# Attention values as two float16 parts with a power-of-two scale per feature, in place of three bfloat16 parts: eight products a head in place of twelve

## The chip, the cores and the metric

The kernel runs on one core of one Trainium2 chip, in one launch. The metric is the device time in microseconds (us) of one execution. Engines are named as in the profile: PE is TensorE (its weight loads are shown apart, as PEld), DVE is VectorE, ACT is ScalarE, POOL is GpSimd and SP is SyncE, which issues most of the DMAs. Each engine works through its own list of instructions in order.

## The reference, cut to what matters

Two layers work on 256 tokens of width 2048 beside 256 context tokens. Layer 0 is a Fourier mixer, layer 1 is attention with 64 query heads over 8 key/value heads of 64 features. The change touches the values of layer 1 alone.

```python
def _attend_with_sink(q, k, v, sink, mask=None):
    s = jnp.einsum('bqhgd,bkhd->bhgqk', q, k).astype(jnp.float32) * (ATTN_HEAD_DIM ** -0.5)
    if mask is not None:
        s = jnp.where(mask, s, NEG_INF)
    sk = jnp.broadcast_to(sink.astype(jnp.float32)[None, :, :, None, None], s.shape[:-1] + (1,))
    p = jax.nn.softmax(jnp.concatenate([s, sk], axis=-1), axis=-1)[..., :-1]
    return jnp.einsum('bhgqk,bkhd->bqhgd', p.astype(v.dtype), v)
...
    y = jnp.moveaxis(o, 0, 1).reshape(b, n, D_BRANCH) * jax.nn.silu(z)
```

All is float32. After attention comes `x + gate * (y @ w_out[1])` and a last norm.

## The kernel before

**Split products.** A float32 product is made of reduced parts. `mm3` (L77 to L80) forms one product of two matrices, each held as a high and a low part (`h`, `l`, or `wh`, `wl`), with three matmuls into one accumulator. The high part is a cast on ACT (L65), the low part a subtraction on DVE (L66). Weights come in 1 MB pieces into `raw` (three buffers) and are split half by half into the pool `ws` (six buffers, so three pairs `wh`, `wl`).

**Keys and values.** With the normed inputs `hx1` (tokens) and `hc1` (context), 32 rounds of products give, for each of four blocks of 128 tokens (`tb` 0 and 1 are tokens, 2 and 3 context), a tile of keys and one of values in PSUM; this takes all eight PSUM buffers. Then the keys of the tokens are rotated (`roped`, L879 to L885, on DVE), those of the context are copied (L941, ACT), and each values tile is split into three bfloat16 parts: a cast on ACT (L930), the rest on DVE (L931), a cast of the rest (L932), a second rest on POOL (L934). The tile `va` (list `v01`) holds parts one and two side by side for each of the eight key/value heads, 64 + 64 columns; `vb` (list `vlo`) holds the third part beside 64 zero columns (L933). At last PE turns the keys (L946, 16 transposes of 128x128) into `kT`.

**The heads.** A loop of 66 turns runs over the 64 query heads. Head i, in `stage_s`, makes its scores with four matmuls of 128x512 (L1134, L1135), takes a masked row maximum on DVE (L1136), the exponential on ACT (L1139), and the scaled probabilities as two float16 parts side by side in `f` (L1146 on ACT, L1147 on DVE). Two DMA transposes (L1148, issued on SP) put `f` into `ft` (three buffers). `stage_o`, two turns later, multiplies `ft` with the values: for each of four key blocks there are three matmuls of 128x256 (L1156: parts one and two times the high probabilities; L1157: the same times the low ones; L1158: part three times the high ones). Rows 0 to 63 and 64 to 127 of the result are added (L1163, L1164), and `emit_y` (L1119) scales by 0.5/PS and gates it.

**What fills PE meanwhile.** Each turn has two slots (`filler`), which take the next unit of a list: the query projections (`q`, 8 units a key/value head), the gate projections (`z`, two units a block) and, once these are used up, 12 units of the output projection (`o`). Ten units run before the first head. A q or z unit is 12 or 16 matmuls; an o unit is half as long. So the last six heads have about half of the filling work of the others.

**What sets the order.** The program is written in this order, but a scheduler with a cost model of its own rearranges it at build time and fixes the order of each engine. A few places are pinned by `issue_after`. The tile pools set when a buffer can be written again.

Of the kernel before, what the change touches and what calls it, by code (L numbers as in the profile page):

```python
# [10 lines left out]
F32 = mybir.dt.float32  # L11
F32R = mybir.dt.float32r
F16 = mybir.dt.float16
BF16 = mybir.dt.bfloat16
AF = mybir.ActivationFunctionType
ALU = mybir.AluOpType
AX = mybir.AxisListType

P = 128
# [4 lines left out]
N = 256  # L24
G = 16
GD = 256
EPS = 1e-6
PS = 32768.0


@with_exitstack
def tile_dit(ctx: ExitStack, tc: tile.TileContext, a: dict, out: bass.AP):
    nc = tc.nc
    V, S, PE, GP = nc.vector, nc.scalar, nc.tensor, nc.gpsimd
# [3 lines left out]
    wsp = ctx.enter_context(tc.tile_pool(name="ws", bufs=6))  # L38
    actp = ctx.enter_context(tc.tile_pool(name="act", bufs=33))
# [3 lines left out]
    def psum():  # L43
        return pp.tile([P, 512], F32, tag="ps", name="ps")
# [9 lines left out]
    def act(dt=F32):  # L54
        return actp.tile([P, 512], dt, tag="act", name="act")
# [44 lines left out]
    ident = const.tile([P, P], F32, name="ident")  # L100
# [452 lines left out]
    for g in range(G):  # L553
# [9 lines left out]
        elif g == 4:  # L563
            w = []
            for kh in range(2):
                with tc.issue_after((mix0, mix1)[kh]):
                    v, m = fold_uh(load_uh(g, kh), g, kh)
# [3 lines left out]
        elif g > 4:  # L571
# [3 lines left out]
            v = f3[1][0]  # L575
# [123 lines left out]
    with tc.tile_pool(name="yp", reuse_waits="tile", bufs=32) as ypool:  # L699
# [20 lines left out]
        with tc.tile_pool(name="zp", reuse_waits="tile", bufs=2) as zp:  # L720
# [30 lines left out]
            for b in range(4, NB):  # L751
# [3 lines left out]
                o = psum()  # L755
# [41 lines left out]
        for i in range(32):  # L797
            sw, kg = i // 16, i % 16
            if kg == 0:
                o = [psum() for _ in range(8)]  # L800
# [6 lines left out]
            if kg >= 12:  # L807
                for k in range(sw * 8 + (kg - 12) * 2, sw * 8 + (kg - 12) * 2 + 2):
                    t = act()
# [41 lines left out]
    with tc.issue_after(st_end[0]):  # L851
        o = psum()
# [33 lines left out]

    with tc.tile_pool(name="h1", reuse_waits="tile", bufs=16) as h1p:
        hx1 = []
        v01, vlo = [], []
        kT = []  # L890
        with tc.tile_pool(name="kvp", reuse_waits="tile", bufs=2) as kvp:
            hc1 = []
            for k in range(KT):
                hx = h1p.tile([P, 512], F32R, tag="h1", name="h1")
                hc = kvp.tile([P, 512], F32R, tag="h1c", name="h1c", bufs=16)
                t = kvp.tile([P, 512], F32, tag="ht", name="ht")
                for s, h in ((0, hx), (1, hc)):
                    q = slice(s * N, (s + 1) * N)
                    V.scalar_tensor_tensor(t[:, q], x1[k][:, q], gs1[:, k, s : s + 1], r_bc1[:, q] if k else r_ps[s], op0=ALU.mult, op1=ALU.mult)
                    a_ = S.activation(h[:, 0:N], t[:, q], AF.Identity, bias=sh1[:, k, s : s + 1]).ins  # L900
                    if s == 0:
                        a_end = a_
                    e = V.scalar_tensor_tensor(h[:, N : 2 * N], t[:, q], sh1[:, k, s : s + 1], h[:, 0:N].bitcast(F32), op0=ALU.add, op1=ALU.subtract).ins
                if k == 0:
                    h_end = [e] + [S.copy(r_bc1[:, i * N : (i + 1) * N], r_ps[i]) for i in range(2)]
                    with tc.issue_after(bc_end), tc.issue_after(a_end):
                        x1_turn(0, 3)
                        x1_turn(1, 3)
                hx1.append(hx)
                hc1.append(hc)  # L910
            o = [[psum() for _ in range(2)] for _ in range(4)]
            for kg in range(8):
                with tc.issue_after(h_end[0]), tc.issue_after(sq_end[0]):
                    w = ws_split(raw(a["wkv"][kg])) if kg else [w0, half_split(wr, 1)]
                for j in range(2):
                    k = kg * 2 + j
                    wh, wl = w[j]
                    for tb in range(4):
                        h = (hx1, hc1)[tb // 2][k]
                        c = (tb % 2) * P  # L920
                        for kv in range(2):
                            q = slice(kv * 512, (kv + 1) * 512)
                            mm3(o[tb][kv], h[:, c : c + P], h[:, N + c : N + c + P], wh[:, q], wl[:, q], k == 0, k == KT - 1)
            kr = []
            for tb in range(4):
                src = o[tb][1].rearrange("p (h d) -> p h d", d=64)
                va, vb = (actp.tile([P, 8, P], BF16, tag="act", name="v") for _ in range(2))
                rest = act()
                rv = rest.rearrange("p (h d) -> p h d", d=64)
                S.copy(va[:, :, 0:64], src)  # L930
                V.tensor_tensor(rv, src, va[:, :, 0:64], op=ALU.subtract)  # L931
                S.copy(va[:, :, 64:128], rv)  # L932
                GP.memset(vb[:, :, 64:128], 0.0)  # L933
                GP.tensor_tensor(vb[:, :, 0:64], rv, va[:, :, 64:128], op=ALU.subtract)  # L934
                v01.append(va)
                vlo.append(vb)
                t = kvp.tile([P, 512], F32, tag="kr", name="kr", bufs=4)
                if tb < 2:
                    roped(t, o[tb][0], tb, kvp)
                else:  # L940
                    S.copy(t, o[tb][0])  # L941
                kr.append(t)
            for hp in range(4):
                o = psum()
                for tb in range(4):
                    PE.transpose(o[:, tb * P : (tb + 1) * P], kr[tb][:, hp * P : (hp + 1) * P], ident)  # L946
                t = act()
                S.copy(t, o)
                kT.append(t)


        y1 = []
        raw1, fin = [None], []
        oA, curw, kg1, yh = [], [None], [0], []
        with tc.tile_pool(name="at", reuse_waits="tile", bufs=2) as at:

            kk, qq, obs, szs = {}, {}, {}, {}
# [155 lines left out]
            def emit_y(blk):  # L1113
                if blk not in szs or (blk, 1) not in obs or blk in ydone:
                    return
                ydone.add(blk)
                if blk % 2 == 0:
                    y1.append(act())
                V.scalar_tensor_tensor(y1[blk // 2][:, (blk % 2) * N : (blk % 2 + 1) * N], obs[blk, 1], 0.5 / PS, szs.pop(blk), op0=ALU.mult, op1=ALU.mult)  # L1119

            def stage_s(i):
                hk, blk, hh = i // 8, i // 2, i % 2
# [28 lines left out]
            def stage_o(i, ft):  # L1151
                hk, blk, hh = i // 8, i // 2, i % 2
                oo = psum()
                for kb in range(4):
                    fh, fl = (ft[:, j, :, :].rearrange("p t q -> p (t q)") for j in (kb, 4 + kb))
                    PE.matmul(oo[:, 0:N], v01[kb][:, hk, :], fh, start=kb == 0, stop=False)  # L1156
                    PE.matmul(oo[:, 0:N], v01[kb][:, hk, :], fl, start=False, stop=False)  # L1157
                    PE.matmul(oo[:, 0:N], vlo[kb][:, hk, :], fh, start=False, stop=kb == 3)  # L1158
                if hh == 0:
                    obs[blk, 0] = at.tile([P, N], F32, tag="ob", name="ob", bufs=4)  # L1160
                ob = obs[blk, 0]
                t = at.tile([64, N], F32, tag="ot", name="ot", bufs=1)
                S.copy(t, oo[64:128, 0:N])  # L1163
                V.tensor_tensor(ob[hh * 64 : hh * 64 + 64, :], oo[0:64, 0:N], t, op=ALU.add)  # L1164
                if hh == 1:
                    obs[blk, 1] = ob
                    emit_y(blk)
# [27 lines left out]
        with tc.tile_pool(name="fin", reuse_waits="tile", bufs=1) as fp:  # L1195
# [31 lines left out]
            o = [[psum() for _ in range(2)] for _ in range(2)]  # L1227
# [182 lines left out]
```

## Time and profile before

| | |
|---|---|
| median of 3 runs | 1826.32 us (1824.57 to 1828.72) |
| the profiled execution | 1825.82 us, its span 1823.8 us |
| PE busy | 1783.1 us (98%) |
| DVE busy | 1407.4 us (77%) |
| ACT busy | 900.6 us (49%) |
| key and value products end | about 1115 us |
| first head's scores, last head's values product | 1156 us, 1665 us |

Times in the trace count from the start of the span. A row of a timeline gives the start and the duration in us, the engine, the line and what is written from what; a bracket gives the idle time of the engine before it and who ended it. A PE row's duration includes its pipeline, so what a matmul costs in a dense stretch is the distance from one start to the next. In a table of groups, "x256 | 71.3, 279 | 12.0" is 256 instructions, 71.3 us busy, 279 ns each, and 12.0 us of idle time just before them. A table by windows gives for each stretch the busy time of each engine, the granted clock of PE, and the busy share of the DMA engines.

### The profile page before, as it was taken

What the parts mean: (1) busy time and instruction counts of PE and PEld (TensorE: products, weight loads), DVE (VectorE), ACT (ScalarE), POOL (GpSimd) and SP (SyncE); (2) the same over time, 40 slices, a digit from 0 to 9 for tenths busy, and PEclk for the clock granted to TensorE, in tenths of its full rate; (3) what the DMA queues carried; (4) which work ended last, traced back from release to release, by engine and by line L of the source; (5) the groups of instructions that cost most, each with busy time, mean ns of one, the idle gap of its engine ahead of it and who ended that gap; (6) DMA issues with size and microseconds to landing.
All of it is one profiled execution on the core that took longest, in us unless ns stands there. A gap on an engine that the chain in (4) does not pass through costs nothing. (4 is left out here: it accounts for less than half of the span.)

```text
span 1823.8 us, 26431 instructions
## 1 busy us (share of the span) xinstructions
PE 1783.1 (98%) x9661; PEld 1501.0 (82%) x9661; DVE 1407.4 (77%) x2774; ACT 900.6 (49%) x1535; POOL 187.0 (10%) x193
## 2 busy tenths in 40 slices
PE   6999999999999999999999999999999999997997
PEld 4679999888888888888888888788888888886886
DVE  5779888887879887767874745889889988995455
ACT  5545444522222243324322534788778877875343
POOL 0001112000000000000000002203221220300001
PEclk9999999999999999999999999999999999998999
DMA  9988889665766647653566333687888798986553
GB/s 395 417 326 236 232 242 254 220 223 225 259 237 242 241 170 294 245 208 118 193 255 257 117 113 117 185 205 191 200 203 203 200 207 193 247 199 194 187 183 138
DMA packets 209473, 399.93 MB, mean 219 GB/s; under 512 B 156288, under 2 KB 156688, under 8 KB 174272
## 3 DMA queue, kind: packets, MB, share of 16 engines
q1 hardware_dynamic: 185280, 360.24, 61.7%
q0 software_dynamic: 19920, 31.06, 6.8%
q10 hardware_dynamic: 4144, 6.95, 1.1%
q8 instruction: 76, 1.25, 0.3%
q14 instruction: 53, 0.43, 0.1%
HBM read 352.06 MB, written 12.59 MB: 200 GB/s over the span
## 5 line engine op out<-in xcount | busy, mean ns | idle before, releaser
L65 ACT CAST wh<-raw 128x1024 fp32r<-128x1024 f32 x333 | 348.9, 1049 | 565.1 <-PE ps L79 447.6
L66 DVE TENSOR_TENSOR wl<-raw,wh 128x1024 fp32r<-128x1024 f32 x333 | 422.6, 1271 | 240.5 <-ACT wh L65 237.1
L79 PE MATMUL ps<-act,wh 128*128 128x512 f32 x1024 | 398.2, 389 | 0.0
L78 PE MATMUL ps<-act,wh 128*128 128x512 f32 x1024 | 393.7, 389 | 0.0
L80 PE MATMUL ps<-act,wl 128*128 128x512 f32 x1024 | 392.8, 389 | 0.0
L80 PEld LDWEIGHTS ps<-act,wl 128*128 128x128 f32 x1024 | 192.2, 188 | 39.9
L79 PEld LDWEIGHTS ps<-act,wh 128*128 128x128 f32 x1024 | 192.2, 188 | 39.8
L78 PEld LDWEIGHTS ps<-act,wh 128*128 128x128 f32 x1024 | 192.2, 188 | 39.7
L1098 PE MATMUL ps<-h,wh 128*128 128x512 f32 x512 | 185.8, 400 | 0.0
L686 DVE CUSTOM_DVE_ANT_0 raw<-raw,cb 128x512 f32<-128x512 f32 x256 | 172.7, 689 | 13.0 <-DMA raw<-in_adw 9.5
L686 DVE CUSTOM_DVE_ANT_0 junk<-raw,cb 128x512 f32<-128x512 f32 x192 | 132.1, 688 | 24.2 <-DMA raw<-in_adw 12.9
L1100 PE MATMUL ps<-h,wl 128*128 128x256 f32 x512 | 138.2, 280 | 0.0
L78 PE MATMUL ps<-wh,h 128*128 128x512 f32 x320 | 125.7, 398 | 0.0
L79 PE MATMUL ps<-wl,h 128*128 128x512 f32 x320 | 124.9, 390 | 0.0
L80 PE MATMUL ps<-wh,h 128*128 128x512 f32 x320 | 124.0, 390 | 0.0
L1098 PEld LDWEIGHTS ps<-h,wh 128*128 128x128 f32 x512 | 96.2, 188 | 20.0
L1147 DVE SCALAR_TENSOR_TENSOR f<-p,sm,f 128x512 f16<-128x512 f32 x128 | 99.1, 807 | 11.9 <-ACT f L1146 11.4
L1139 ACT ACTIVATE p<-ps,mx 128x512 f32<-128x512 f32 x128 | 87.8, 687 | 36.5 <-DVE mx L1136 35.4
L1136 DVE CUSTOM_DVE_ANT_0 ps<-ps,mask,nsink 128x512 f32<-128x512 f32 x128 | 92.9, 752 | 9.6 <-PE ps L1135 9.0
L1100 PEld LDWEIGHTS ps<-h,wl 128*128 128x128 f32 x512 | 96.7, 189 | 2.6
L1146 ACT ACTIVATE f<-p,sm 128x512 f16<-128x512 f32 x128 | 87.6, 717 | 20.5 <-DMA ft<-f 18.7
L1156 PE MATMUL ps<-ft,v 128*128 128x256 f16 x256 | 71.3, 279 | 12.0 <-DMA ft<-f 9.8
(325 smaller groups left out, 3461.2 us busy)
## 6 DMA issues: line engine op xcount, KB each, us to landing
raw<-in_wz SPq DMA_DIRECT2D x64, 1024.0 KB, 5.5
raw<-in_adw SPq DMA_DIRECT2D x64, 1024.0 KB, 4.9
raw<-in_awp SPq DMA_DIRECT2D x32, 1024.0 KB, 12.8
raw<-in_wo SPq DMA_DIRECT2D x32, 1024.0 KB, 6.1
raw<-in_wq SPq DMA_DIRECT2D x32, 1024.0 KB, 5.4
raw<-in_wu SPq DMA_DIRECT2D x32, 1016.0 KB, 6.0
raw<-in_wo1b SPq DMA_DIRECT2D x16, 1024.0 KB, 4.9
act<-in_xT POOLq DMA_DIRECT2D x32, 256.0 KB, 6.6
```

What stands on the lines that cost most here:

```text
L65: last_cast[0] = S.copy(h, src).ins
L66: last_sub[0] = V.tensor_tensor(l, src, h.bitcast(F32), op=ALU.subtract).ins
L78: PE.matmul(o, wh, xh, start=start, stop=False)
L79: PE.matmul(o, wh, xl, start=False, stop=False)
L80: return PE.matmul(o, wl, xh, start=False, stop=stop).ins
L686: V.tensor_tensor_reduce(junk if s == 0 and i < 3 else wf, wf, cb[:, s, kq * 512 : kq * 512 + 512], 1.0, 0.0, ALU.mult, ALU.add, acc[:, i, ...
L1098: PE.matmul(o[0], wh[:, q], hx1[k], start=k == 0, stop=k == KT - 1)
L1100: PE.matmul(o[0][:, 0:N], wl[:, q], hx1[k][:, 0:N], start=False, stop=False)
L1136: V.tensor_tensor_reduce(o, o, mask[:, tb, :], -0.125, nsink[:, i : i + 1], ALU.add, ALU.min, mx[:, tb : tb + 1])
L1139: S.activation(pt[tb], so[tb], AF.Exp, bias=mx[:, tb : tb + 1], scale=-1.0, accum_out=sm[:, tb : tb + 1])
L1146: S.activation(f[:, 0:512], pt[tb], AF.Copy, scale=sm[:, tb : tb + 1])
L1147: V.scalar_tensor_tensor(f[:, 512:1024], pt[tb], sm[:, tb : tb + 1], f[:, 0:512], op0=ALU.mult, op1=ALU.subtract)
```

## The change

The values are split into two float16 parts in place of three bfloat16 parts, so `vb` and one matmul in three go. For float16 to hold them, each of the 512 features (8 heads by 64) is first multiplied by a power of two, found at run time: the sum of the absolute values of the feature over all 512 tokens comes from four matmuls with a tile of ones (`oner`), so that every partition has it; DVE takes its exponent with shifts and adds on the bits, makes the factor `up_` (applied to the values) and its inverse `dn`, with 1/PS and the 0.5 of the gate in it. Eight PE transposes turn `dn` so that the inverse stands one value a partition, in `dsc`, and `emit_y` multiplies by a column of `dsc` in place of the constant.

```diff
-        v01, vlo = [], []
+        v01, vs = [], []
+        dsc = h1p.tile([P, 8], F32, name="dsc", bufs=1)
...
+            oner = kvp.tile([P, P], F32R, name="oner", bufs=1)
+            S.activation(oner, ident, AF.Identity, bias=1.0, scale=0.0)
...
-                src = o[tb][1].rearrange("p (h d) -> p h d", d=64)
-                va, vb = (actp.tile([P, 8, P], BF16, tag="act", name="v") for _ in range(2))
-                rest = act()
-                rv = rest.rearrange("p (h d) -> p h d", d=64)
-                S.copy(va[:, :, 0:64], src)
-                V.tensor_tensor(rv, src, va[:, :, 0:64], op=ALU.subtract)
-                S.copy(va[:, :, 64:128], rv)
-                GP.memset(vb[:, :, 64:128], 0.0)
-                GP.tensor_tensor(vb[:, :, 0:64], rv, va[:, :, 64:128], op=ALU.subtract)
-                v01.append(va)
-                vlo.append(vb)
+                t, ab = act(), act(F32R)
+                S.copy(t, o[tb][1])
+                S.activation(ab, o[tb][1], AF.Abs)
+                vs.append((t, ab))
...
+            l1 = psum()
+            for tb in range(4):
+                PE.matmul(l1, oner, vs[tb][1], start=tb == 0, stop=tb == 3)
+            l1s, up_, ex = act(), act(), act(I32)
+            V.tensor_scalar(l1s, l1, 2.0**-96, None, op0=ALU.max)
+            V.tensor_scalar(ex, l1s.bitcast(I32), 23, None, op0=ALU.logical_shift_right)
+            V.tensor_scalar(up_.bitcast(I32), ex, -1.0, 268.0, op0=ALU.mult, op1=ALU.add)
+            V.tensor_scalar(up_.bitcast(I32), up_.bitcast(I32), 23, None, op0=ALU.logical_shift_left)
+            V.tensor_scalar(ex, ex, -30.0, None, op0=ALU.add)
+            dn = wsp.tile([P, 8, 2, 64], F32, tag="ws", name="dn")
+            V.tensor_scalar(dn.bitcast(I32), ex.rearrange("p (h d) -> p h d", d=64).unsqueeze(2).broadcast_to([P, 8, 2, 64]), 23, None, op0=ALU.logical_shift_left)
+            for half in range(2):
+                o = psum()
+                for j in range(4):
+                    PE.transpose(o[:, j * P : (j + 1) * P], dn[:, half * 4 + j].rearrange("p c d -> p (c d)"), ident)
+                V.tensor_copy(dsc[:, half * 4 : half * 4 + 4], o[:, 0::P])
+            for tb in range(4):
+                t = vs[tb][0]
+                va = actp.tile([P, 8, P], F16, tag="act", name="v")
+                tv = t.rearrange("p (h d) -> p h d", d=64)
+                V.tensor_tensor(t, t, up_, op=ALU.mult)
+                S.copy(va[:, :, 0:64], tv)
+                GP.tensor_tensor(va[:, :, 64:128], tv, va[:, :, 0:64], op=ALU.subtract)
+                v01.append(va)
...
-                V.scalar_tensor_tensor(y1[blk // 2][:, (blk % 2) * N : (blk % 2 + 1) * N], obs[blk, 1], 0.5 / PS, szs.pop(blk), op0=ALU.mult, op1=ALU.mult)
+                V.scalar_tensor_tensor(y1[blk // 2][:, (blk % 2) * N : (blk % 2 + 1) * N], obs[blk, 1], dsc[:, blk // 4 : blk // 4 + 1], szs.pop(blk), op0=ALU.mult, op1=ALU.mult)
...
                     PE.matmul(oo[:, 0:N], v01[kb][:, hk, :], fh, start=kb == 0, stop=False)
-                    PE.matmul(oo[:, 0:N], v01[kb][:, hk, :], fl, start=False, stop=False)
-                    PE.matmul(oo[:, 0:N], vlo[kb][:, hk, :], fh, start=False, stop=kb == 3)
+                    PE.matmul(oo[:, 0:N], v01[kb][:, hk, :], fl, start=False, stop=kb == 3)
```

Up to the key and value products the order of every engine stays as it was. Three places behind them move.

The first is PE just behind the last key and value product (`h1c` is the context's input, `kr` the keys to be transposed, `h` the tokens' input in the first query projection). Before:

```order
L79 MATMUL ps<-wl,h1c 128x512
L80 MATMUL ps<-wh,h1c 128x512
L946 MATMUL ps<-ident,kr 128x128 x4
L78 MATMUL ps<-wh,h_9254 128x512
L79 MATMUL ps<-wl,h_9254 128x512
L80 MATMUL ps<-wh,h_9254 128x512
L78 MATMUL ps<-wh,h_9281 128x512
```

Now:

```order
L79 MATMUL ps<-wl,h1c 128x512
L80 MATMUL ps<-wh,h1c 128x512
L942 MATMUL ps<-ident,kr 128x128 x4
L949 MATMUL ps<-act,oner 128x512 x2
L942 MATMUL ps<-ident,kr 128x128 x8
L949 MATMUL ps<-act,oner 128x512
L942 MATMUL ps<-ident,kr 128x128 x4
L949 MATMUL ps<-act,oner 128x512
L961 MATMUL ps<-ident,dn 128x128 x8
L78 MATMUL ps<-wh,h_9257 128x512 x2
L79 MATMUL ps<-wl,h_9257 128x512
```

Before, the query projection went on behind four transposes, and the other twelve came later, between its matmuls; now all sixteen, the four products with ones and the eight transposes of `dn` stand ahead of it.

The second is DVE at the same place. Before:

```order
L879 TENSOR_TENSOR kr<-ps,rope 128x512
L884 TENSOR_TENSOR rt<-ps,rope 128x16x16 x2
L66 TENSOR_TENSOR wl<-raw,wh 128x1024
L931 TENSOR_TENSOR act<-ps,v 128x512
L879 TENSOR_TENSOR kr<-ps,rope 128x512
L884 TENSOR_TENSOR rt<-ps,rope 128x16x16
L885 TENSOR_TENSOR kr<-kr,rt 128x512
```

Now, from the last rotation on:

```order
L885 TENSOR_TENSOR kr<-kr,rt 128x512
L951 TENSOR_SCALAR act<-ps 128x512
L952 TENSOR_SCALAR act<-act 128x512
L953 TENSOR_SCALAR act<-act 128x512
L954 TENSOR_SCALAR act<-act 128x512
L955 TENSOR_SCALAR act<-act 128x512
L967 TENSOR_TENSOR act<-act 128x512 x4
L957 TENSOR_SCALAR dn<-act 128x1024
L66 TENSOR_TENSOR wl<-raw,wh 128x1024 x2
L962 COPY dsc<-ps 128x4 x2
```

The four multiplications of the values (L967) stand ahead of `dn` (L957), and the first two weight splits of the query projection stand behind it.

The third is ACT around the last three heads (`ot` is a head's values product being drained, `act` and `ys` are parts of the gated result, `wh` are weights of the output projection). Before:

```order
L1163 COPY ot<-ps 64x256
L1139 ACTIVATE p,sm<-ps,mx 128x512 x2
L1140 ACTIVATE es<-mx,sink 128x2
L1163 COPY ot<-ps 64x256
L1146 ACTIVATE f<-p,sm 128x512 x2
L65 CAST act<-act 128x256 x8
L1163 COPY ot<-ps 64x256
L65 CAST wh<-raw 128x1024
L1163 COPY ot<-ps 64x256
L65 CAST wh<-raw 128x1024
```

Now:

```order
L1182 COPY ot<-ps 64x256
L1166 ACTIVATE f<-p,sm 128x512 x2
L65 CAST act<-act 128x256 x8
L1159 ACTIVATE p,sm<-ps,mx 128x512
L1166 ACTIVATE f<-p,sm 128x512 x2
L65 CAST wh<-raw 128x1024 x2
L1182 COPY ot<-ps 64x256
L65 CAST wh<-raw 128x1024 x2
L1182 COPY ot<-ps 64x256
```

Now the last head's probabilities stand behind the eight casts, and more output projection work lies between the last values products: on PE there are 48 of its matmuls between the last head's scores and its values product, where there were 22.

More of the change, by code (lines that the diff above doesn't have):

```diff
@@ L13 @@
 F16 = mybir.dt.float16
-BF16 = mybir.dt.bfloat16
 AF = mybir.ActivationFunctionType
@@ L28 @@
 PS = 32768.0
+I32 = mybir.dt.int32
 @with_exitstack
```

## The prediction

> **What bounds the kernel now.** I read the page first, then windows over the stage of the heads, then its waits.
>
> ```profile
> PE 1783.1 (98%) x9661; PEld 1501.0 (82%) x9661; DVE 1407.4 (77%) x2774; ACT 900.6 (49%) x1535; POOL 187.0 (10%) x193
> L1156 PE MATMUL ps<-ft,v 128*128 128x256 f16 x256 | 71.3, 279 | 12.0 <-DMA ft<-f 9.8
> ...
> 1200.00:1600.00 400.00, 400.00 (x2291) 336.20 (x2289) 357.33 (x665) 317.49 (x611) 88.28 (x68) 1.00 0.86 206
> 1646.00:1656.00 10.00, 0.32 (x3) 0.04 (x1) 3.98 (x12) 3.59 (x9) 1.06 (x2) 0.67 0.99 301
> ```
>
> Where the changed products run (1200 to 1600 us) PE has work in all of 400 us, DVE in 357.33 (89%), ACT in 317.49 (79%), the DMA engines in 0.86. PE stands still only at the end of that stage, for nearly ten microseconds. The waits of 1200 to 1600 say who has slack:
>
> ```profile
> DVE wl L66 <- ACT wh L65: 21.7, 33, 1.1
> ACT wh L65 <- PE ps L79: 13.0, 24, 1.3
> ACT f L1146 <- DMA ft<-f: 12.6, 15, 2.0
> ACT wh L65 <- PE ps L1100: 11.7, 18, 1.3
> DVE ps L1136 <- PE ps L1135: 8.3, 16, 0.8
> ```
>
> ACT's weight casts wait for PE to give a buffer back (13.0 and 11.7 us), DVE for ACT's casts and PE's scores. The splits run ahead of PE. PE is the bound here, but DVE is only 43 us of 400 behind it.
>
> **Products removed.** What a product costs is the distance of starts:
>
> ```profile
> 1404.77 0.27 PE L1156 MATMUL ps<-ft,v 128*128 128x256 f16 x1
> 1404.88 0.27 PE L1157 MATMUL ps<-ft,v 128*128 128x256 f16 x1
> 1411.04 0.39 PE L79 MATMUL ps<-wl,h 128*128 128x512 f32 x1
> 1411.27 0.39 PE L80 MATMUL ps<-wh,h 128*128 128x512 f32 x1
> ```
>
> A values product costs 0.11 us (not the 279 ns of the group, which contains the pipeline), a 512-wide one 0.23. Four fewer a head are 0.44 us; 58 heads with full filling work give 58 x 0.44 = 25.5 us. The last six are counted below.
>
> Does the rest of a head follow? Head 32 begins its scores at 1400.14, head 33 at 1407.87: 7.73 us a head.
>
> ```profile
> 1400.14 0.39 PE L1134 MATMUL ps<-kkh,qa 128*128 128x512 f32 x1
> 1407.87 0.39 PE L1134 MATMUL ps<-kkh,qb 128*128 128x512 f32 x1
> 1408.81 3.83 SPq L1148 DMA_TRANSPOSE ft<-f  x1
> DMA to landing us min/median/max: 2.0/5.3/10.6
> 1419.23 0.28 PE L1156 MATMUL ps<-ft,v 128*128 128x256 f16 x1
> ```
>
> Its second transpose is issued at 1408.81, lands about 5.3 us later (the median) at 1414.1, and the values product starts at 1419.23: 5.1 us in hand. Two turns and a bit shorten that by about 1 us. Only the late landings (up to 10.6) would then hold PE. DVE's 357.33 us would fall into 400 - 51 x 0.44 = 377.6 us (51 heads lie in that window), 95%, and the DMA share goes from 0.86 to 0.91. The bounds of what is given back in the heads are 0 and the whole 25.5 (if DVE or the transposes hold the old pace); I take 3 us, near the lower end, since the slack of 5 us and the splits' lead outlast most delays.
>
> **The scale, at the seam between the value products and the query projection.** Durations are from these rows:
>
> ```profile
> 1112.70 0.58 ACT L930 CAST v<-ps 128x512 bf16<-128x512 f32 x1 [0.78 <-PE ps L80]
> L930 ACT CAST v<-ps 128x512 bf16<-128x512 f32 x4 | 2.4, 591 | 1.3 <-PE ps L80 1.3
> L931 DVE TENSOR_TENSOR act<-ps,v 128x512 f32<-128x512 f32 x4 | 2.6, 678 | 0.0
> L873 DVE TENSOR_SCALAR nsink<-sink 128x64 f32<-128x64 f32 x1 | 0.2, 196 | 0.8 <-DMA sink<-in_sink 0.8
> L1267 DVE TENSOR_SCALAR act<-act,fr 128x256 f32<-128x256 f32 x2 | 0.7, 354 | 0.1
> 1114.57 1.16 POOL L934 TENSOR_TENSOR v<-act,v 128x512 bf16<-128x512 f32 x1 [87.97 <-ACT v L932]
> 1114.60 1.68 DVE L885 TENSOR_TENSOR kr<-kr,rt 128x512 f32<-128x512 f32 x1
> 1117.73 0.68 DVE L885 TENSOR_TENSOR kr<-kr,rt 128x512 f32<-128x512 f32 x1
> 1115.00 0.39 PE L80 MATMUL ps<-wh,h1c 128*128 128x512 f32 x1
> 1116.42 0.63 PE L946 MATMUL ps<-ident,kr 128*128 128x128 f32 x4 [1.04 <-DVE kr L885]
> 1116.81 0.49 PE L78 MATMUL ps<-wh,h 128*128 128x512 f32 x1
> ```
>
> Now PE's last product of the stage starts at 1115.00 and the query projection at 1116.81. In the new order everything on PE goes through `dn`. Step by step: ACT has the second value tile at 1112.70 and from there eight drains of 0.59 (values, absolute values, keys), so the last absolute values are there at 1117.4 and the last product with ones at 1117.8. Then DVE: five TENSOR_SCALAR of 128x512, the four multiplications L967, and `dn` (1024 wide). A TENSOR_SCALAR of 64 takes 196 ns and of 256 354, so the line through both gives 0.56 for 512 and 0.98 for 1024. One from PSUM I take at 0.68. That is 0.68 + 4 x 0.56 + 4 x 0.68 + 0.98 = 6.6 us. It is no less, unless the integer forms run faster than any float row here; doubling the row of 256 gives 7.5, and POOL can add to it: the same DVE operation took 1.68 us beside POOL's L934 and 0.68 alone, and POOL's new subtractions begin as soon as the first L967 is done. With one such collision 7.6, with two and the higher price 9.5. I take 7.6, so `dn` at 1125.4. Eight transposes at 0.39 for four end at 1126.2. Before, with all sixteen key transposes ahead of it, the projection would have begun at 1116.81 + 12 x 0.1 = 1118.0. So it is 8.2 us late, PE's twelve added matmuls included. The weight splits queued behind `dn` (L66, 1.27 us) end at about 1126.7, while PE still does its two L78; that costs nothing.
>
> PE then starts at half clock, as it does after its other two stalls:
>
> ```profile
> 1656.10 0.37 PE L1156 MATMUL ps<-ft,v 128*128 128x256 f16 x1 [9.78 <-DMA ft<-f]
> 1656.27 0.42 PE L1157 MATMUL ps<-ft,v 128*128 128x256 f16 x1
> 1659.78 0.40 PE L79 MATMUL ps<-wl,act 128*128 128x512 f32 x1
> 1167.84 0.27 PE L1156 MATMUL ps<-ft,v 128*128 128x256 f16 x1 [2.18 <-ACT f L1146]
> 1171.71 0.39 PE L1098 MATMUL ps<-h,wh 128*128 128x512 f32 x1
> ```
>
> From 1656.10 to 1659.78 it did 12 values products and four wide ones, 12 x 0.11 + 4 x 0.23 = 2.2 us of work, in 3.7: 1.5 us lost, and 1.6 after the stall of 2.18. The seam costs 8.2 + 1.5, say 10 us; bounds 7.5 and 13. [...]
>
> Work that hides under PE: ACT's four casts L930 and four L932 become eight drains and four casts; POOL's memsets go; the pointer `dsc` in place of a constant at L1119. None waits for the path beyond what is counted. Nothing changes ahead of the seam. The first head's wait (2.18 us above) stays, since it hangs on that head's own softmax.
>
> **The last six heads.** There PE has little filler and waits for transposes:
>
> ```profile
> 1638.81 0.48 PE L1134 MATMUL ps<-kkh,qa 128*128 128x512 f32 x1
> 1643.81 0.48 PE L1134 MATMUL ps<-kkh,qb 128*128 128x512 f32 x1
> 1664.10 0.28 PE L1156 MATMUL ps<-ft,v 128*128 128x256 f16 x1
> ```
>
> Heads 62 and 63 begin their scores at 1638.81 and 1643.81, and the last values product begins at 1664.10; between lie 22 output matmuls and the idle 9.78 us. In the new order 48 stand there, so 26 x 0.23 = 5.9 us of work that followed now fits into that idle time. The four products fewer of each of these heads mostly shorten waits. I take -6; bounds 0 (the last `f` stands behind eight casts on ACT now and may land later by as much) and -7.5.
>
> **Sum**, against the profiled execution, 1825.82 us (its span 1823.8 and 2.0 around it, half a microsecond below the median of 1826.32): -25.5 + 3 + 10 - 6 = -18.5, so **1807 us**. The likeliest case's own range, with 0 to 8 back in the heads, is 1798 to 1819.
>
> **Rivals.**
> - *The seam is cheap or the tail fills wholly:* 7.5, -7.5 and nothing back: 1825.8 - 25.5 = 1800. For it: DVE is empty when the chain starts. Against it: POOL.
> - *Half of the heads' gain goes back* in waits for late landings and for DVE at 95%, with a seam of 12: -12.7 + 12 - 5 = 1820. For it: the 43 us of DVE idle time are mostly waits that don't vanish.
> - *The heads keep their pace, set by `ft`* (slower side). If softmax, transposes or DVE, and not PE, end each turn, PE waits 0.44 us a head more and gains nothing: 0 + 10 - 6 = +4, or +10 with a tail of no gain: 1830 to 1836. It decides once the landing of head i slips more than the 5.1 us in hand. Against it: PE is never idle in 400 us and ACT waits for PE.
> - *Float16 values load slowly.* The trace has float32 and bfloat16 loads, no float16 ones:
>
> ```profile
> L1098 PEld LDWEIGHTS ps<-h,wh 128*128 128x128 f32 x512 | 96.2, 188 | 20.0
> L1156 PEld LDWEIGHTS <-v 128*128 128x128 bf16 x256 | 25.2, 98 | 26.8 <-issue 13.2 <-DMA ft<-f 10.3 <-DVE mx L1136 0.9
> ```
>
>   At 188 ns eight products take 1.5 us where twelve took 1.32: +0.18 x 64 + 10 = +22, 1848: the change would then not do what it says. Against it: the type is as wide as the one that takes 98. [...]
>
> **How the numbers follow.** Chances: forecast 0.70, cheap seam 0.13, half back 0.09, pace of `ft` 0.06, slow loads 0.02. A measurement can tell about 0.2% (3.7 us) from no change. The first three cases are faster, 0.92; the pace of `ft` lies half within 0.2% and half beyond, so same 0.03, slower 0.05. The range 1798 to 1819 holds most of the forecast and of the cheap seam and a little of the third: about 0.8.
>
> **What would show it.** In the changed profile: values products 0.11 apart and 512 of them; heads at 7.3 us; query projection starting near 1126 with a PE gap of some 7 us that ends on `dn`, and half clock behind it; PE without gaps in the heads; less idle time ahead of the last two values products. It is wrong if PE waits for `ft` or `wl` in most turns, if the gap at `dn` is over 10 us, or if the loads take 188 ns.

## The result, and the profile after

The changed kernel takes 1824.71 us (median of 12 runs, 1820.38 to 1826.94), the kernel before 1826.58 beside it (12 runs): a ratio of 0.9991, 95% interval 0.9983 to 0.9998. That is inside the 0.2% that can be told from no change; forecast were 1807 us and a clear gain. The profiled execution was the fastest of the twelve, 1820.38 us with a span of 1818.5, so its profile shows 4.3 us less than the median.

The page's busy times, groups by line (busy us, mean ns of one, idle before), and the window over the heads:

```profile
PE 1769.2 (97%) x9417; PEld 1480.0 (81%) x9417; DVE 1411.1 (78%) x2782; ACT 896.2 (49%) x1540; POOL 188.7 (10%) x189
```

```profile
L1176 PE MATMUL ps<-ft,v 128*128 128x256 f16 x256 | 60.5, 276 | 11.3 <-DMA ft<-f 11.3
L1177 PEld LDWEIGHTS <-v 128*128 128x128 f16 x256 | 25.2, 99 | 2.4
```

```profile
1200.00:1600.00 400.00, 396.77 (x2185) 329.60 (x2184) 371.51 (x694) 324.60 (x638) 89.18 (x68) 1.00 0.88 215
```

512 values products instead of 768 (x256 on each of two lines), a float16 load takes 99 ns, PE is no longer busy in all of the heads' 400 us, and DVE went from 357.33 to 371.51. The waits of that window show how the slack went:

```profile
PE ps L1176 <- DMA ft<-f: 2.8, 2, 2.1
...
ACT wh L65 <- PE ps L79: 0.9, 1, 0.9
```

ACT's weight casts waited 31 us for PE before (13.0 + 11.7 + 6.3, three rows) and 0.9 now: the splits have no lead left, and PE begins to wait for `ft`.

At the seam, the timeline of PE, that of DVE, and two windows:

```profile
1117.61 0.40 PE L80 MATMUL ps<-wh,h1c 128*128 128x512 f32 x1
1128.13 1.97 PE L961 MATMUL ps<-ident,dn 128*128 128x128 f32 x8 [7.43 <-DVE dn L957]
1129.75 1.20 PE L78 MATMUL ps<-wh,h 128*128 128x512 f32 x2
```

```profile
1120.73 0.69 DVE L951 TENSOR_SCALAR act<-ps 128x512 f32<-128x512 f32 x1 [3.51 <-PE ps L949]
1121.46 0.43 DVE L952 TENSOR_SCALAR act<-act 128x512 int32<-128x512 int32 x1
1123.06 3.45 DVE L967 TENSOR_TENSOR act<-act 128x512 f32<-128x512 f32 x4
1126.43 1.64 DVE L957 TENSOR_SCALAR dn<-act 128x1024 int32<-128x1024 int32 x1
```

```profile
1121.00:1128.00 7.00, 0.00 (x0) 0.00 (x0) 6.90 (x11) 6.22 (x10) 3.51 (x3) 0.84 0.00 0
1128.00:1132.00 4.00, 3.87 (x13) 3.43 (x14) 4.00 (x3) 0.11 (x1) 3.19 (x2) 0.50 0.01 2
```

The gap stands at the place in the order where it was forecast, 7.43 us long and ended by `dn`, with a granted clock of 0.50 behind it (second window). But the last product of the stage before it starts at 1117.61 instead of 1115.00: something ahead of the changed operations had become slower. The same product of the key and value stage (1030 to 1110 us), first before, then after:

```profile
L79 PE MATMUL ps<-wl,h1c 128*128 128x512 f32 x60 | 23.3, 389 | 0.0
```

```profile
L79 PE MATMUL ps<-wl,h1c 128*128 128x512 f32 x57 | 22.5, 396 | 0.0
```

Seven ns more each, and from start to start 226 to 227 ns became 230 to 236. In the output projection (1690 to 1800 us) of the same changed kernel it depends on the tile:

```profile
L79 PE MATMUL ps<-wl,ys 128*128 128x512 f32 x113 | 44.8, 396 | 0.0
L79 PE MATMUL ps<-wl,act 128*128 128x512 f32 x40 | 15.6, 389 | 0.0
```

Slow are the products whose stationary operand is `h1`, `h1c` or `ys`, tiles of the pools that come behind the new 32-byte tile `dsc`; those with an `act` tile, allocated ahead of it, are as before (389 ns).

### The profile page after: what moved, and what is told of

The parts are those of the page before. It is cut to its first block, busy times and chain, and to the rows that moved or that the text cites. A ratio compares the mean times of both kernels' runs of the same rounds, so it can differ in the third digit from the quotient of the medians.

```text
span 1818.5 us, 25947 instructions
## 1 busy us (share of the span) xinstructions
PE 1769.2 (97%) x9417; PEld 1480.0 (81%) x9417; DVE 1411.1 (78%) x2782; ACT 896.2 (49%) x1540; POOL 188.7 (10%) x189
## 5 line engine op out<-in xcount | busy, mean ns | idle before, releaser
L79 PE MATMUL ps<-act,wh 128*128 128x512 f32 x1024 | 398.3, 389 | 0.0
L79 PEld LDWEIGHTS ps<-act,wh 128*128 128x128 f32 x1024 | 192.2, 188 | 39.8
L79 PE MATMUL ps<-wl,h 128*128 128x512 f32 x320 | 127.4, 398 | 0.4 <-DVE wl L66 0.4
L79 PE MATMUL ps<-wl,ys 128*128 128x512 f32 (+1 forms) x192 | 75.1, 391 | 0.0
```

Of the source, the lines that this page charges most:

```text
L79: PE.matmul(o, wh, xl, start=False, stop=False)
```

## The experiments

Differences are between medians. The kernel before ran beside each (1825.76, 1826.83, 1826.72 and 1826.02 us in the four groups of runs). Start addresses are those of the built programs, as remainders modulo 256, which no trace shows: weights, `act`, `h1` and `h1c` at 224 before; `h1` and `h1c` at 0 in the changed kernel, 32 bytes from the weights. Of the 24 `ys` tiles, 16 lie with `h1` and the other eight 64 bytes further on.

### Where the tiles start

**e1** makes `dsc` 64 bytes long, to keep multiples of 64.

```diff
-        dsc = h1p.tile([P, 8], F32, name="dsc", bufs=1)
+        dsc = h1p.tile([P, 16], F32, name="dsc", bufs=1)
```

> The changed kernel with the tile dsc made 64 bytes a partition wide in place of 32, so that all tiles behind it (h1, h1c, ys and those of the attention pool) keep the place within 64 bytes that they had before. Theory A (the 32-byte shift slows the products that take their stationary operand from these tiles from 227 to 232 to 235 ns a start; some 1,700 of them): about 1815 us, key and value products 227 ns apart again. Theory B (nothing but seam and late softmax ate the gain, the slower products are chance of that execution): about 1824 us.

Measured: 1823.85 us, ratio 0.999 (0.998 to 1.0). The products stayed slow (394 ns, 396 in the changed kernel), so here a shift by 64 is hardly better than one by 32; the total says nothing on what the slow products cost. The median is the one that theory B named, and its reason, chance, is wrong: the slow products came again.

```profile
L79 PE MATMUL ps<-wl,h1c 128*128 128x512 f32 x57 | 22.5, 394 | 0.0
```

**e2** gives the kernel before an unused tile of 32 bytes and nothing else.

```diff
+        pad = h1p.tile([P, 8], F32, name="pad", bufs=1)
+        GP.memset(pad, 0.0)
```

> The kernel before with one unused 32-byte tile ahead of h1 and nothing else. Theory A: 8 to 10 us slower than before, about 1835 us, key and value products 232 to 235 ns apart. Theory B: as before, 1826 us, 227 ns.

Measured: 1835.35 us, ratio 1.0057 (1.0045 to 1.0069): 9.6 us slower by a tile that nobody reads.

```profile
L79 PE MATMUL ps<-wl,h1c 128*128 128x512 f32 x57 | 22.5, 395 | 0.0
```

**e5** is the changed kernel with the eight factors in a tile whose contents are dead by then, so that nothing moves.

```diff
-        dsc = h1p.tile([P, 8], F32, name="dsc", bufs=1)
+        dsc = adab.rearrange("p a b c d -> p (a b c d)")[:, 0:8]
```

> The changed kernel with its eight scale factors written into the bias tile adab, which nothing reads any more, so that no new tile is allocated and every tile of the layer-1 pool has the start address that it had in the kernel before. Shift theory: what slowed the 512-wide products whose stationary operand lies in that pool is that they no longer start at the same place within 512 bytes as the tiles that stream past them (both at 224 of 512 before; 0 against 224 in the changed kernel, 32 against 224 with the tile of 64 bytes, which did not help). Then the key/value and query products start 227 ns apart again where they started 232 to 235 apart, the output products too, and the median falls by about what the same shift cost the kernel before (9.6 us): 1824.7 - 9.6 = 1815. Rival, heads' theory: the pitch comes back, but the heads run at the pace of the transposed probabilities, and PE's waits for ft grow by what the products give: 1821 to 1825. Rival, no address: the pitch stays at 232 or more and the median at 1824.

Measured: 1820.2 us, ratio 0.9961 (0.9948 to 0.9973). The products are back at 389 ns; the median fell by 4.5 us where 9.6 were expected. The traces show where: the first scores come 3.9 us earlier (1165.65 against 1169.57), in the heads little came of it (the scores of heads 8 and 48 start 298.46 us apart in the changed kernel, 298.05 here), and from the scores of head 56 to the end nothing (232.6 and 232.9 us), where e2 had lost 5.5 (239.8 against 234.3). From head 56's scores to the last head's values product the mean clock was 0.91 in e5 and 0.95 in the changed kernel. (The addresses in the expectation, 224, 0 and 32, are remainders modulo 256, not 512.)

```profile
L79 PE MATMUL ps<-wl,h1c 128*128 128x512 f32 x60 | 23.3, 389 | 0.0
```

**e12** shifts everything by 32 bytes, weights and layer-1 tiles alike.

```diff
+    cpad = const.tile([P, 8], F32, name="cpad")
+    GP.memset(cpad, 0.0)
     cc = cload("cc", [P, KT, 2], nc.sync)
```

> The kernel before with an unused tile of 32 bytes in the first pool, so that every later tile, weights and layer-1 pool alike, starts 32 bytes further on (0 mod 512 where it was 224 + a multiple of 256). If the pitch of the 512-wide products depends on where the stationary operand starts against the operand that streams past it, it stays 226 to 227 ns, and the time is that of the kernel before, 1826. If it depends on the start address of the stationary operand alone (slow at 0 and 32 mod 512), all such products go to 232 ns or more, those of layer 0 as well: 1845 or more.

Measured: 1826.13 us, ratio 1.0 (0.9988 to 1.0012), and 389 ns. `h1` starts at the same addresses here and in e2 (395 ns), so its own address alone doesn't make the products slow; what differs between the two runs is where it starts against the weights that stream past it, level here and 32 bytes off there. The kernel before fits that: its eight `ys` tiles at 32 stand 64 bytes from the weights, and the output products between 1750 and 1770 us, which use them, have a mean of 398 ns, those between 1700 and 1720 us, on the other tiles, 389 (both L79).

```profile
L79 PE MATMUL ps<-wl,h1c 128*128 128x512 f32 x60 | 23.4, 389 | 0.0
```

### The scale search

**e3** (64-byte `dsc`) and **e6** (addresses as before) leave the search out: no column sums, no exponents, the values split unscaled, constant factors. What is left is eight products a head.

```diff
-            l1 = psum()
...
+            GP.memset(dsc, 0.5 / PS)
...
-                V.tensor_tensor(t, t, up_, op=ALU.mult)
```

> dsc 64 bytes wide, and the search for the scale left out: values are split into two float16 parts unscaled, dsc is a constant. That leaves out the column sums, the exponents and the multiplication of the values. Theory A: about 1805 us (10 below the run with the wide dsc, which is the price of the seam). Theory B: about 1813 us.

> The changed kernel without the scale search (no column sums, no exponents, the factors a constant, the values split unscaled into two float16 parts), all start addresses as in the kernel before. This is eight products a head and nothing else. The sum of the prediction for it: 1825.8 - 25.5 + 3 given back in the heads - 6 in the last six heads = 1797. Heads' theory (the gain is there, but the tail behind the last head gives back): the last scores come at about 1622 us of the profile against 1643.81 before, and the end at 1800 to 1803. Rival, pace of ft: PE waits for ft in every head, 1808 or more.

Measured: e3 1811.78 us, ratio 0.9931 (0.9918 to 0.9945); e6 1805.95, ratio 0.9883 (0.9868 to 0.9898), between the expected 1800 to 1803 and the rival's 1808. Against e5 the search costs 14.2 us in the medians (e1 against e3: 12.1); in the profiled executions the first scores come at 1165.65 with it and at 1155.73 without, 9.9 us. The profiled execution of e5 was its fastest, that of e6 its slowest. Where the rest comes from is open: the five runs of e5 show mean granted clocks of 0.991 to 0.992, those of e6 0.994 to 0.995, but the profiled run of e5 has 0.992 as well.

**e4** (64-byte `dsc`) and **e7** (addresses as before) move the search into the first query projection, in two pieces; **e8** cuts it into eight.

```diff
             for i in range(first):
                 emit_unit()
+                if i == 1:
+                    ex_ = scale_a()
+                if i == 4:
+                    scale_b(ex_)
```

> dsc 64 bytes wide, the whole computation kept, but the search for the scale written behind the second unit of the query projection, and the exponent of dn and its transposes behind the fifth, so that PE has work while DVE finds it. If the seam costs 10 us by PE's wait for dn: about 1806 us with theory A, 1814 with B, no PE gap on dn. If the seam's price is DVE's and ACT's time rather than the wait: 1812 or more with A.

> The changed kernel with the scale search moved into the query projection of the first head (column sums and exponents behind its second piece, the factors' transposes behind its fifth), all start addresses as in the kernel before. Shift theory and seam theory add: 1819.1 with the 64-byte tile, less 9 to 10 for the pitch, 1809 to 1811. Rival, heads' theory: 1816 to 1819.

> As the one before, but the scale search is cut into eight pieces, one behind each of the pieces 1 to 8 of the first query projection, so that no DVE piece of it over 1.5 us stands ahead of a weight split. In the kernel with it in two pieces PE waited 4.3 us for a weight split behind the chain of the exponents. Seam theory: that wait is gone, and the half clock behind it too: 4 to 6 us under the kernel with two pieces, 1804 to 1806, and within 4 us of the kernel without the search. Rival: the search's DVE work of some 13 us has no room in the 28 us of the projection beside the weight splits, and PE waits as much in smaller portions: no less than the kernel with two pieces.

Measured: e4 1819.11 us, ratio 0.9967 (0.9955 to 0.9979); e7 1812.7, 0.9921 (0.9908 to 0.9935); e8 1811.43, 0.9916 (0.9903 to 0.993). All three missed: e4 was expected at 1806 or 1814, e7 at 1809 to 1811, e8 at 1804 to 1806. e7 is 7.5 us under e5, somewhat less than expected: PE still waits 4.5 us for a weight split, and e8 did not mend it: the scheduler put the pieces together again, and its PE wait is the same 4.5 us. The PE wait and the DVE timeline of e7:

```profile
PE ps L79 <- DVE wl L66: 4.5, 1, 4.5
```

```profile
1126.14 1.52 DVE L1170 TENSOR_SCALAR act<-act 128x512 int32<-128x512 int32 x1
1127.69 1.40 DVE L1171 TENSOR_SCALAR act<-act 128x512 int32<-128x512 int32 x1
1129.13 1.40 DVE L1172 TENSOR_SCALAR act<-act 128x512 int32<-128x512 int32 x1
1130.44 1.51 DVE L1184 TENSOR_SCALAR act<-act 128x512 int32<-128x512 int32 x1
1131.88 3.45 DVE L1177 TENSOR_TENSOR act<-act 128x512 f32<-128x512 f32 x4
1135.25 2.17 DVE L66 TENSOR_TENSOR wl<-raw,wh 128x1024 fp32r<-128x1024 f32 x1
```

Nine us without a weight split, and the operations take 1.40 to 1.52 us where they took 0.43 in the changed kernel. The trace of e4 has them at 1.40 to 1.53, with POOL's split of the keys beside them (1127.41 to 1133.99).

**e9** takes both away: the search starts ahead of the first piece, its parts are pinned behind weight splits, the factors' exponents go into `act` tiles, and POOL's key split waits until piece 5.

```diff
+                if i == 0:
+                    scale(i)
                 emit_unit()
-                scale(i)
+                if i:
+                    with tc.issue_after(last_cast[0]), tc.issue_after(last_sub[0]):
+                        scale(i)
...
-                    if (n, i) == (0, 3):
+                    if (n, i) == (0, 5):
```

> All start addresses as in the kernel before; the column sums and the five exponent operations stand ahead of the first query piece, the four multiplies of the values behind its pieces 1 to 4, each behind a weight split, the factors' exponents behind piece 6 in two tiles that take no weight buffer, their transposes behind piece 8, and the split of the keys for the first head (POOL) waits until piece 5. In the two kernels before this one the exponent operations took 1.40 to 1.53 us each beside POOL's key split, where they take 0.43 alone, and all of the chain stood in one stretch of 9 us without a weight split, whatever the order of the program text, so PE waited 4.5 us. Seam theory: without POOL beside them and with the splits between them the wait is below 1 us, and the half clock behind it is gone: 1806 to 1808, within 2 us of the kernel without the search (1805.95). Rival: the search costs what its DVE work costs wherever it stands, 1811 as in the one before.

Measured: 1808.42 us (1805.67 to 1810.07), ratio 0.9903 (0.989 to 0.9917), the whole computation. First scores at 1157.08, 1.4 us behind the kernel without a search (2.5 us in the medians, where at most 2 were expected), and PE has no wait from 1110 to 1160 us. It changes the start, the splitting and POOL's place at once, so which of them did it is not shown. Its DVE timeline:

```profile
1124.12 0.42 DVE L1172 TENSOR_SCALAR act<-act 128x512 int32<-128x512 int32 x1
1124.57 0.43 DVE L1173 TENSOR_SCALAR act<-act 128x512 int32<-128x512 int32 x1
1124.92 1.22 DVE L66 TENSOR_TENSOR wl<-raw,wh 128x1024 fp32r<-128x1024 f32 x1
```

This version beats both kernels.

### The heads and the last turns

**e10** is e9 with 18 instead of 12 row blocks of the output projection in the heads' loop.

```diff
-                for k in range(12):
+                for k in range(18):
...
                 filler()
+                if i >= 60:
+                    filler()
```

> As the one before, with 18 instead of 12 of the output projection's row blocks done inside the heads' loop, the six more of them in the last six turns, three pieces a turn instead of two. Tail theory: in the last heads PE has only 2.7 us of output products a turn beside 1.9 us of scores and values, while the softmax takes 7 us a head, so the products that the change saves there become waiting time; six more blocks are 36 products of 0.227 us, 8.2 us of work moved into that time: 4 to 8 us faster than the kernel before this one, 1799 to 1804. Rival, softmax pace: the weight casts and splits that these blocks bring (1.05 + 1.22 us for half a weight tile on ACT and DVE) stand ahead of the softmax of the last heads and make it later by as much: no difference, or slower, 1806 or more.

Measured: 1813.45 us, ratio 0.9931 (0.9918 to 0.9945), 5 us slower than e9. It didn't test its theory: the scheduler left the last turns alone (29 output products between the scores of head 63 and the last values product, 30 in e9). The loss lies between the scores of heads 48 and 56, 69.4 us apart where e9 has 62.8: a wait of 6.0 us for a late `ft`, in a stretch (1541 to 1581 us) where the mean clock is 0.91 and the DMA engines are busy 98% of the time. Why `ft` was later than in e9 (2.5 us of such waits there) is open.

```profile
PE ps L1152 <- DMA ft<-f: 6.0, 1, 6.0
```

**e11** is e6 with four products a head, those with the low halves of the probabilities left out.

```diff
-                    PE.matmul(oo[:, 0:N], v01[kb][:, hk, :], fh, start=kb == 0, stop=False)
-                    PE.matmul(oo[:, 0:N], v01[kb][:, hk, :], fl, start=False, stop=kb == 3)
+                    PE.matmul(oo[:, 0:N], v01[kb][:, hk, :], fh, start=kb == 0, stop=kb == 3)
```

> The kernel without the scale search and with the start addresses of the kernel before, less four more products a head: the products with the low halves of the probabilities are left out. If the heads run at PE's pace, each of the 48 heads between the 8th and the 56th gives another 4 x 0.11 = 0.44 us: 7.53 to 7.09 us a head, 21 us in all. Theory of the first and last heads: the first eight heads (55.1 us in both kernels so far) and the last six run at the softmax's pace and give nothing, so the sum is at most 21 of the 25.5. Rival, pace of DVE and ft: DVE is busy 373 of 400 us, 7.0 us a head, and the transposes land 1.3 to 2 us ahead of their use, so the period stops at 7.2 to 7.4 and the heads give 6 to 15 us: 1791 to 1800.

Measured: 1831.99 us, ratio 1.003 (1.0018 to 1.0041). With 256 products less it is 26 us slower than e6, and both theories were wrong in the sign. Its waits and window (1200 to 1600 us):

```profile
PE ps L1157 <- DMA ft<-f: 38.5, 17, 10.6
```

```profile
1200.00:1600.00 400.00, 360.86 (x1837) 297.31 (x1836) 359.72 (x650) 307.98 (x599) 88.08 (x68) 0.97 0.82 202
```

PE now waits for late probabilities 17 times, up to 10.6 us, and its mean clock over the window is 0.97, in e6 1.00: the work of heads 8 to 48 keeps it busy for 289.6 us, in e14 for 280.6.

**e13** halves the transposes of e11, **e14** also leaves out DVE's operation that makes the low halves.

```diff
-                    V.scalar_tensor_tensor(f[:, 512:1024], pt[tb], sm[:, tb : tb + 1], f[:, 0:512], op0=ALU.mult, op1=ALU.subtract)
-                    nc.sync.dma_start_transpose(ft[:, :, tb, :], f)
+                    nc.sync.dma_start_transpose(ft[:, 0:4, tb, :], f[:, 0:512])
```

> The kernel with four products a head and no scale search, whose two transposes a head now carry only the high halves of the probabilities (the low halves, which nothing multiplies there, are still made by DVE). Transposes' theory: if the DMA queues make the probabilities late, PE's waits for ft (38.5 us between 1200 and 1600) fall below 10 and the median from 1832 to 1790 or less. DVE's theory: DVE's rows are the same, so the waits stay above 25 us and the median above 1820.

> As the one before, and DVE doesn't make the low halves at all (two operations of 0.75 us a head less, about 80 us in the stage of 1200 to 1600). DVE's theory: only now do the waits for ft go, and the heads come at PE's pace, 7.89 - 8 x 0.11 = 7.0 us a head: 1785 to 1793. Transposes' theory: no different from the one before by more than 4 us.

Measured: e13 1809.0 us, ratio 0.9909 (0.9894 to 0.9925); e14 1768.37, ratio 0.9682 (0.9666 to 0.9699). First e13's waits and window, then those of e14:

```profile
PE ps L1157 <- DMA ft<-f: 20.5, 9, 7.9
```

```profile
1200.00:1600.00 400.00, 378.91 (x1954) 312.83 (x1953) 369.50 (x684) 321.68 (x638) 88.61 (x68) 0.97 0.64 176
```

```profile
PE ps L1156 <- DMA ft<-f: 10.4, 1, 10.4
```

```profile
1200.00:1600.00 400.00, 389.57 (x2055) 323.72 (x2054) 317.31 (x633) 346.01 (x681) 81.11 (x69) 0.99 0.70 197
```

e13 lies between its two theories (1790 or less, 1820 or more), e14 further down than DVE's theory had it (1785 to 1793). With the bytes of the transposes halved, the waits fall by about half (38.5 to 20.5 us), and the DMA engines' share goes from 0.82 to 0.64. The rest goes with DVE's operation: the one wait of e14, 10.4 us, stands behind the last head's scores. Only then do the heads come at PE's pace. In e14 the scores of heads 8 and 56 start at 1202.42 and 1539.24: 336.82 / 48 = 7.02 us a head, which is 7.89 - 8 x 0.11 as expected; the first eight heads fall too, from 55.07 to 46.20 us. In e6 it was 7.53, in e11 7.99. DVE's operation was not taken away alone, so whether its time on DVE or its place in the chain to `f` matters is not shown, nor is why e11 is slower than e6 and not only no faster.

## Why the prediction was wrong

By its own terms, each against the kernel before in the same group of runs (changed kernel -1.9, e5 -6.6, e6 -20.9):

| term | forecast | measured | from |
|---|---|---|---|
| start addresses | 0 | +4.8 | changed kernel against e5 |
| the seam | +10 | +14.2 | e5 against e6 |
| heads and last turns | -28.5 | -20.9 | e6 |
| sum | -18.5 | -1.9 | |

**"Nothing changes ahead of the seam"** failed. The diff was read for its operations and not for its allocations: a tile of 32 bytes moved every later tile against the weights. It costs 9.6 us on the kernel before (e2) and 4.8 here; with a `dsc` of 64 bytes, against the kernel before of each group, 6.9 (e3 against e6) and 7.5 (e4 against e7). Why it is less here than in e2 is open. It also delayed the seam by 2.6 us (1115.00 to 1117.61).

**The seam:** the mechanism and its place were right. From the first DVE operation (1120.73) to `dn` (1128.07) it took 7.3 us, forecast 7.6: the integer forms were cheaper (0.43, forecast 0.56), the multiplications, partly beside POOL, dearer (0.86 each in the mean, forecast 0.68 with one collision), and `dn`, beside POOL, too (1.64, forecast 0.98; in e8 0.69). So the near agreement of the sum is in part luck: its terms were off both ways. (Doubling the row of 256 gives 7.65, not 7.5, in the prediction's own sum.) PE's start at half clock was a term too small: a clock of 0.50 was granted from 1125.8 to 1132.6, and PE worked at it for 4.5 us, so by estimate half of that, 2.3 us, was lost where 1.5 stood. In the traces the search costs 9.9 us, as forecast; what the medians add is open. The seam is not a price of the method: e9 pays 1.4 us at the first scores.

**The heads:** "I take 3 us, near the lower end, since the slack of 5 us and the splits' lead outlast most delays" is the step that failed here. From the first scores to those of head 56, e6 gained 17.3 us in its profile (433.81 to 416.52), where the sum holds 56 x 0.44 - 3 = 21.6: 7.3 us were given back instead of 3. (In the profiles e6 is 18.0 us under the kernel before: 0.0 up to the first scores, these 17.3, and 0.7 behind them.) The starts of both heads, before and in e6:

```profile
1155.75 0.39 PE L1134 MATMUL ps<-kkh,qa 128*128 128x512 f32 x1
1589.56 0.39 PE L1134 MATMUL ps<-kkh,qa 128*128 128x512 f32 x1
```

```profile
1155.73 0.39 PE L1135 MATMUL ps<-kkh,qa 128*128 128x512 f32 x1
1572.25 0.40 PE L1135 MATMUL ps<-kkh,qa 128*128 128x512 f32 x1
```

Waits of PE make up 5.6 of the 7.3 (2.2 us before, 7.8 in e6; the rest is not traced). First those of e6 for the first eight heads, then those up to head 56 (0.4 and 0.2 us come to these):

```profile
PE ps L1157 <- ACT f L1147: 3.6, 2, 2.2
```

```profile
PE ps L1157 <- DMA ft<-f: 3.6, 2, 2.9
```

They are few. Between the scores of heads 8 and 48 PE is still busy for 297.1 of 298.4 us, and a head takes 7.46 us where it took 7.89; some 13 query products, 3 us of PE's work, are done earlier now. The first eight heads take 55.08 us, before 55.07, with 12 such products more and a new wait of 1.5 us for `f`. Heads 48 to 56 hold the same work but for the values products, and gain 0.2 us of the 3.5 that were forecast: PE's busy time falls from 63.2 to 60.1, and one wait of 2.9 us for `ft` takes that back. There the DMA engines, which also bring weights and other data (`raw<-in_wz`, `act<-x1d`), are busy 100% of the time, before 96%. That this made `ft` late was not tried.

ACT's waits for PE, the splits' lead, went from 31 to 0.9 us in the changed kernel, so the lead was not slack that stays; behind it DVE is at 93%. e11, e13 and e14 show how near the limit is: with four products a head fewer yet the time rose, and it fell only when transposes and DVE work were taken away. That is shown for four products a head; that the lost lead caused the waits of e6 is argued. The rival "the heads keep their pace, set by `ft`" describes heads 48 to 56, not the 40 heads before them, and it priced the limit as a lost gain, where e11 shows that it can be a loss.

**The last six heads:** "I take -6" failed too. 48 output products stand where 22 stood, as forecast, but almost nothing was gained: from the scores of head 56 to the end e6 takes 233.6 us, before 234.3. In e6 PE waits 10.9 us there (7.5 + 2.0 + 0.8 + 0.6) where it waited 9.8, and from head 56's scores to the last head's values product its mean clock is 0.91, before 0.93. ACT's timeline of e6 shows how:

```profile
1627.67 0.30 ACT L1141 ACTIVATE es<-mx,sink 128x2 f32<-128x2 f32 x1 [0.96 <-DVE mx L1137]
1634.36 0.37 ACT L1163 COPY ot<-ps 64x256 f32<-64x256 f32 x1 [6.39 <-PE ps L1158]
1634.63 1.33 ACT L1147 ACTIVATE f<-p,sm 128x512 f16<-128x512 f32 x2
```

The probabilities `f` of head 62 stand behind the copy of head 61's result, which waits for PE, which waits for head 61's `ft`: each head waits for the one before it, and more products on PE don't shorten that. That this order is the whole reason was not tried.

**Float16 loads** of 128x128 take 98 to 99 ns in the changed kernel, as the bfloat16 ones did before, while float32 ones take 188 in both: that rival is gone.

## What to carry to other kernels

Read a diff for its allocations too: a new small tile ahead of large ones moves all of them, and a compare of one untouched product's duration in a stage ahead of the change (389 against 396 ns) shows it at once. Put small tiles into dead space (e5), or, which was not tried here, behind the large ones. Where, as here, the bound engine is busy in 400 of 400 us and the next in 357, don't count the time that the others wait for the bound engine as slack: 31 us of it went to 0.9 with one saving, and the next saving (e11) made the kernel slower. Price the last turns of a loop apart from its middle: here the middle gave most of its share, and from head 48's scores to the end of the kernel less than 1 us was gained (297.5 to 296.6). Measure work at a seam apart from the steady state as well, and start it where its engine is idle (e9).

## What was not expected of the hardware

- In the key and value stage a 128x512 float32 product takes 389 ns, and in the kernel before 226 to 227 from start to start, in the runs where its stationary operand and the streamed weights have the same start address modulo 256 (before, e5, e12). It takes 394 to 396 ns, and in the changed kernel 230 to 236 from start to start, where they are 32 or 64 bytes apart (changed kernel, e2, e1). The load of the stationary operand stays at 188 ns (before and changed kernel). That 256 is the modulus that counts is not shown. Where `h1` streams past stationary weights (the gate products) it isn't so: their mean is 400 ns before, 397 in the changed kernel and 404 in e5, and what decides there is open.
- An integer TENSOR_SCALAR of 128x512 on DVE took 0.42 to 0.43 us with POOL idle (changed kernel, 1121.46 to 1123.15; POOL starts at 1124.49) and 1.40 to 1.53 beside a POOL subtraction (e4), 3.3 to 3.6 times as long.
- At the seam the clock of 0.50 came 5.1 us after PE had gone idle (1120.7 to 1125.8) in the changed kernel and 4.2 us in e5. It stayed through 4.5 us of work in the one and 3.6 in the other.
- With the transposed bytes halved (e11 to e13), the DMA engines' busy share went from 0.82 to 0.64 and about half of PE's waits for `ft` (38.5 to 20.5 us) went with it, though these engines were not full on average.
